# A hybrid decoder layer on one core: key scales applied later, the first six up blocks reordered, weight sums of four blocks made in DRAM

## The chip, the cores and the metric

The kernel runs on one core of a Trainium2 chip. The metric is the device time of one execution in microseconds (us). The core has five engines with a program each: TensorE (PE, whose weight loads are shown apart as PEld), VectorE (DVE), ScalarE (ACT), GpSimd (POOL) and SyncE (SP). Each works through its instructions strictly in order; an instruction that waits holds up all that stand behind it on that engine. Transfers are issued from a queue of SP, ACT or POOL and run on 16 DMA engines that the queues share. [...]

## The reference

One layer on 512 tokens of width 2048, in fp32. The kernel computes all of it; these lines are the ones around the change.

```python
def rwkv7_mix(zs, ...):
    ...
    kk = (k * k_k).reshape(hd).astype(f32)
    kk = kk / jnp.maximum(jnp.sqrt(jnp.sum(kk * kk, axis=-1, keepdims=True)), 1e-12)
    ...
def conv_ffn(h, w_up, conv_w, conv_b, w_down):
    u = h @ w_up
    ...
    val, gate = jnp.split(c, 2, axis=-1)
    return (jax.nn.silu(gate) * val) @ w_down

def reference(x, ...):
    h = rms_norm(x, norm1_g[l])
    z = h @ w_in[l]
    ...
    o_rw = rwkv7_mix(...)
    o_att = swa_attention(...)
    ...
    x = x + (g_rw * p_rw + g_att * p_att) @ w_out[l]
    x = x + conv_ffn(rms_norm(x, norm2_g[l]), w_up[l], conv_w[l], conv_b[l], w_down[l])
```

## The kernel before

**Precision.** Every fp32 operand of a large product is split into a high part (an ACT copy to fp32r, `whi` for weights) and a low part (a DVE subtraction, `wlo`), and a product is made of three matmul passes: high by high, high by low, low by high.

**Stages, in order of time.** Input projection and attention (to about 310 us); eight pairs of RWKV heads, some 98 us each, with the remaining columns of the projection filling TensorE between the steps of the recurrence (to 1100); gates and branch projection (to 1329); the output projection "o" (to 1489); "up" (1490 to 2404); "down" (to 2829). The three last matrices go through a two-by-two scheme with seven products in place of eight. In "up" these are P1, P2, P7, P6, P5, Q4 and P3 for each of 44 blocks of weight columns; each product is 24 matmuls of 128x128 by 128x256. A product needs its weight as a sum of quarters of the block: s1 and s3 are sums of two quarters, P6 and P3 of three and four. It needs also its own form of the activations, a difference of the quarters q11 to q22 that is split into high and low parts on the spot (b11, b21, t3, t2, t1, t4, b22; `split_q`, L1033 to L1035).

**Weight sums in DRAM.** For "o" and "down" the sums are made in DRAM long before: `sums_along` (L226) takes a job, SP copies one quarter (L230) and POOL accumulates the other on it (L231), once per so many weight loads of the projection. For "up" the sums are made on chip: a POOL accumulate onto the loaded tile (L1056) for s1 and s3, and a DVE addition (`sums`, L1063) for P6 and P3.

**A pair of RWKV heads.** `early(p + 1)` computes the operands of the next pair while `late(p)` runs the recurrence of this one. In `early`, `head_rows` (L329) turns 8 row factors per token tile into rows that all partitions have: a PE transpose, a DVE copy to `rsT` (L332), a DMA to DRAM (`rsd`, L334) and two broadcast DMAs back (`rsb`, L338), all on SP. DVE then multiplies the keys with them (`kk`, L552). In `late`, each of the eight steps of the recurrence runs psG (PE, L731), GY (DVE, L732), psU (PE, L734), UV (ACT and DVE, L735 and L736), psS (PE, L740), SV (DVE, L744). POOL clears BAR for the next pair (L754).

**What sets the order.** Instructions are emitted under a planner that orders free ones by its own costs; those passed to `pin` keep their place. In "up" the list `steps` sets the order of the products; `run(i)` prepares the weights of product i + 2 (`prep`, which calls `parts`: whi L1069, wlo L1070), runs the matmuls of product i (L1087) and calls `out`, which moves finished sums from PSUM to `u` (ACT L1103, DVE L1105 and L1107). There are two `u` tiles for alternating blocks, and `conv` (L1121 to L1129) reads them; its parts wait in the list `later` and are handed out one or two per product.

For the first four blocks the order before is P1 of all four, P2 of all four, P7 of all four, and then the rest of blocks 0 and 1, and of 2 and 3. P1 is kept in an SBUF tile `t1`; P2 stays in the Z half of the block's X bank until `out("P2")` adds it to `t1` into `u`, after twelve products for blocks 0 and 1 and later still for 2 and 3:

```python
    for f in range(2):
        B[f].out("P2")
    for i in range(3 * NPRE, len(steps)):
        run(i)
        if steps[i] in ((2, "P6"), (2, "Q4")):
            B[2 + (steps[i][1] == "Q4")].out("P2")
```

## Time and profile before

| | |
|---|---|
| median of 3 runs | 2829.64 us (2828.12 to 2833.07) |
| profiled execution | 2830.7 us, of which the span of the instructions 2828.9 |
| mean granted TensorE clock | 0.996 |
| PE busy | 2774.4 us, 98% of the span, 17450 instructions |
| DVE, ACT, POOL busy | 1987.5 (70%), 1342.1 (47%), 225.1 (8%) |
| DMA, shares of 16 engines | SP's queue 47.1% (432.64 MB), POOL's 24.5% (132.14 MB) |

A row of a group names line, engine, operation, tiles, then the busy time, the mean of one in ns, and the idle time before it with what ended it. A row of waits names who waited for whom, the total, the number and the longest. A row of a timeline gives start, duration and instruction. "SPq" and "POOLq" are the DMA queues' issuing instructions; a transfer lands later. TensorE is the engine to follow: with 98% busy, time is won or lost where it stops or runs at a lower granted clock.

### The profile page before, as it was taken

The page shows a single profiled execution, that of the slowest core. Times are in us where ns is not written, and L with a number is a line of the kernel's source. Part 1 is how long each engine was busy: PE and PEld are TensorE (multiplying, and loading weights), DVE is VectorE, ACT ScalarE, POOL GpSimd, SP SyncE. Part 2 cuts the span into 40 slices and gives each one's busy share as a digit, 9 for nine tenths or more (in the row PEclk, how much of TensorE's full clock was granted, in tenths as well). Part 3 has the DMA queues.
Part 4 walks back from the last instruction along what each step waited for, and adds up shares of the span by engine and source line. Part 5 has one row for each costly group of instructions (what it writes and reads, how often), then busy time and mean ns, then how long its engine had stood idle before and what let it go on. Part 6 is the DMA issues. An engine that isn't in the chain of part 4 may idle for free.

```text
span 2828.9 us, 45923 instructions
## 1 busy us (share of the span) xinstructions
PE 2774.4 (98%) x17450; PEld 2403.0 (85%) x17450; DVE 1987.5 (70%) x3437; ACT 1342.1 (47%) x2256; POOL 225.1 (8%) x299
## 2 busy tenths in 40 slices
PE   7999999999999999999999899999999999999999
PEld 5777777777777777888888899999999999888887
DVE  4588677777777774545678777878787878655555
ACT  4355445444544553322465455555545555444444
POOL 0001000000000001011010011011101110000000
PEclk9999999999999999999999999999999999999999
DMA  7865766666666667878777789888988897877775
GB/s 216 227 159 163 187 167 168 175 164 158 175 162 171 160 165 223 234 248 292 237 251 211 210 235 241 229 229 227 241 236 222 228 242 228 315 245 241 256 256 190
DMA packets 223726, 607.04 MB, mean 215 GB/s; under 512 B 24448, under 2 KB 44560, under 8 KB 222480
## 3 DMA queue, kind: packets, MB, share of 16 engines
q1 hardware_dynamic: 156096, 432.64, 47.1%
q0 software_dynamic: 36064, 132.14, 24.5%
q10 hardware_dynamic: 31344, 39.31, 4.0%
q8 instruction: 137, 2.24, 0.3%
q14 instruction: 85, 0.70, 0.1%
HBM read 554.38 MB, written 174.40 MB: 258 GB/s over the span
## 4 chain that ended last, share of the span: by engine, by line
PE 87%; DVE 5%; ACT 3%; DMA 2%; issue 1%; SPq 0%; POOL 0%; ACTq 0%; DVEq 0%; POOLq 0%
PE X L1087 18%; PE X L954 11%; PE acc L256 9%; PE acc L255 9%; PE acc L257 9%; PE Y L954 9%; PE Y L1087 9%; PE Z L1087 4%; DVE wlo L241 1%; PE psS L740 1%; PE psG L731 1%; PE bulk L623 1%; PE bulk L673 1%; PE bulk L534 1%; ACT whi L240 1%
## 5 line engine op out<-in xcount | busy, mean ns | idle before, releaser
L255 PE MATMUL acc<-xhi,whi 128*128 128x512 f32 x1152 | 462.9, 402 | 1.9 <-DVE xlo L301 1.9
L257 PE MATMUL acc<-xhi,wlo 128*128 128x512 f32 x1152 | 463.8, 403 | 0.0
L256 PE MATMUL acc<-xlo,whi 128*128 128x512 f32 x1152 | 462.2, 401 | 0.0
L947 DVE TENSOR_TENSOR wlo<-raw,whi 128x1024 fp32r<-128x1024 f32 x210 | 256.9, 1224 | 205.1 <-ACT whi L946 204.9
L240 ACT ACTIVATE whi<-raw 128x512 fp32r<-128x512 f32 x352 | 220.0, 630 | 375.7 <-PE acc L256 295.1
L946 ACT ACTIVATE whi<-raw 128x1024 fp32r<-128x1024 f32 x210 | 222.8, 1061 | 290.6 <-PE X L954 152.9
L241 DVE TENSOR_TENSOR wlo<-raw,whi 128x512 fp32r<-128x512 f32 x352 | 241.3, 689 | 167.1 <-ACT whi L240 146.9
L1087 PE MATMUL X<-b,whi 128*128 128x256 f32 x1472 | 270.2, 284 | 2.3 <-DVE u L1107 0.9
L1087 PE MATMUL X<-t,whi 128*128 128x256 f32 x1408 | 259.6, 285 | 10.3 <-DVE u L1107 9.8
L1070 DVE TENSOR_TENSOR wlo<-raw,whi 128x1024 fp32r<-128x1024 f32 x176 | 215.0, 1222 | 77.6 <-ACT whi L1069 77.3
L1087 PE MATMUL Y<-t,whi 128*128 128x256 f32 x1408 | 257.1, 283 | 0.0
L255 PEld LDWEIGHTS acc<-xhi,whi 128*128 128x128 f32 x1152 | 217.6, 189 | 43.4 <-issue 2.5
L256 PEld LDWEIGHTS acc<-xlo,whi 128*128 128x128 f32 x1152 | 217.5, 189 | 41.9 <-issue 3.3
L257 PEld LDWEIGHTS acc<-xhi,wlo 128*128 128x128 f32 x1152 | 217.5, 189 | 38.3 <-issue 1.1
L1069 ACT ACTIVATE whi<-a 128x1024 fp32r<-128x1024 f32 x132 | 139.3, 1056 | 216.5 <-DVE a L1063 214.3
L1087 PEld LDWEIGHTS X<-b,whi 128*128 128x128 f32 x1472 | 230.7, 193 | 3.1 <-issue 2.4
L1087 PEld LDWEIGHTS X<-t,whi 128*128 128x128 f32 x1408 | 221.6, 194 | 10.9 <-DVE u L1107 7.2
L1087 PEld LDWEIGHTS Y<-t,whi 128*128 128x128 f32 x1408 | 219.8, 192 | 0.0
L1087 PE MATMUL X<-b,wlo 128*128 128x256 f32 x736 | 209.3, 284 | 2.1 <-DVE wlo L1070 2.1
L1070 DVE TENSOR_TENSOR wlo<-a,whi 128x1024 fp32r<-128x1024 f32 x132 | 161.7, 1226 | 67.3 <-ACT whi L1069 66.7
L1087 PE MATMUL X<-t,wlo 128*128 128x256 f32 x704 | 200.4, 285 | 0.0
L1087 PE MATMUL Y<-t,wlo 128*128 128x256 f32 x704 | 199.4, 283 | 0.0
(339 smaller groups left out, 5762.1 us busy)
## 6 DMA issues: line engine op xcount, KB each, us to landing
raw<-in_w_up_dram SPq DMA_DIRECT2D x180, 512.0 KB, 4.6
raw<-in_w_z_dram SPq DMA_DIRECT2D x288, 256.0 KB, 3.9
s_dn<-in_w_dn_dram POOLq DMA_DIRECT2D x88, 512.0 KB, 5.9
raw<-in_w_up_dram POOLq DMA_DIRECT2D x88, 512.0 KB, 8.7
raw<-s_dn SPq DMA_DIRECT2D x88, 512.0 KB, 3.8
raw<-in_w_dn_dram SPq DMA_DIRECT2D x66, 512.0 KB, 3.5
a<-in_w_up_dram SPq DMA_DIRECT2D x48, 512.0 KB, 6.9
s_dn<-in_w_dn_dram SPq DMA_DIRECT2D x44, 512.0 KB, 4.9
```

The source lines that it names most:

```text
L240: act.activation(hi, raw, AF.Copy)
L241: dve.tensor_tensor(lo, raw, hi.bitcast(F32), op=ALU.subtract)
L255: pe.matmul(acc, whi[:, j], xhi[:, k], start=first, stop=False)
L256: pe.matmul(acc, whi[:, j], xlo[:, k], start=False, stop=False)
L257: pe.matmul(acc, wlo[:, j], xhi[:, k], start=False, stop=last)
L534: pe.matmul(ps, w[:, i], ads[:, i], start=i == lo, stop=i == hi - 1)
L946: act.activation(whi, wr, AF.Copy)
L947: dve.tensor_tensor(wlo, wr, whi.bitcast(F32), op=ALU.subtract)
L954: pe.matmul(dst, l[:, q, ts], r[:, es], start=fst and j == 0, stop=lst and j == 2, skip_group_check=True)
L1069: pin(act.activation(hi, t, AF.Copy))
L1070: pin(dve.tensor_tensor(lo, t, hi.bitcast(F32), op=ALU.subtract))
L1087: pin(pe.matmul(ps, l[:, k], r[:, k], start=start and k + i == 0, stop=last and i == 2, skip_group_check=True))
```

## The change

**Weight sums of four up blocks.** For blocks 0 to 3 the four sums s3, s1, P6 and P3 are made in DRAM (`up_d`), 16 jobs in all. `up_sum` issues one job after each of the three gates of a pair: two transfers of 512 KB on POOL's queue, a plain copy and an accumulate that waits for the copy. In "up" these blocks load the finished sums with SP; their POOL accumulates and DVE additions are gone. On POOL's queue, around the first pair's gates (s1_dn and s3_dn are sums of "down", BAR the memset of L754), stood before:

```order
L231 DMA s4_o2_100<-in_w_o_dram 128x1024 x2
L231 DMA s4_o3_101<-in_w_o_dram 128x1024 x2
L231 DMA s1_dn0_102<-in_w_dn_dram 128x1024
L231 DMA s3_dn0_124<-in_w_dn_dram 128x1024
L231 DMA s1_dn0_102<-in_w_dn_dram 128x1024
L754 MEMSET BAR_2910 64x8x64 x2
L231 DMA s3_dn0_124<-in_w_dn_dram 128x1024
```

and stands now:

```order
L239 DMA s4_o2_100<-in_w_o_dram 128x1024 x2
L239 DMA s4_o3_101<-in_w_o_dram 128x1024 x2
L245 DMA s3_u0_146<-in_w_up_dram 128x1024 x2
L239 DMA s1_dn0_102<-in_w_dn_dram 128x1024
L245 DMA s1_u0_147<-in_w_up_dram 128x1024 x2
L239 DMA s3_dn0_124<-in_w_dn_dram 128x1024
L245 DMA P6_u0_148<-in_w_up_dram 128x1024
L245 DMA P6_u0_148<-s1_u0_147 128x1024
L239 DMA s1_dn0_102<-in_w_dn_dram 128x1024
L766 MEMSET BAR_2926 64x8x64 x2
L239 DMA s3_dn0_124<-in_w_dn_dram 128x1024
```

Each job's copy and accumulate stand behind a sum of "down" and ahead of the next one.

**Key scales.** The multiplication of `kk` with the row factors is pinned behind three operations of the value's path. On DVE, for pair 1, with the recurrence of pair 0 around it (kz is the key's tile, k2 and lw other operands of the pair), stood before:

```order
L744 SCALAR_TENSOR_TENSOR SV_2917<-SV_2917,ee_3240,psS_3630 64x64 x2
L583 TENSOR_SCALAR k2_4041<-lw_3883,half_175 128x512
L584 TENSOR_TENSOR k2_4041<-k2_4041,kz_3827 128x512
L732 COPY GY_2919<-psG_3659 128x128
L552 TENSOR_TENSOR kk_3830<-kk_3830,rsb_3861 128x512
L585 TENSOR_SCALAR lw_3883<-lw_3883 128x512
L736 COPY UV_2918<-psU_3663 64x64
L587 TENSOR_TENSOR kz_3827<-kk_3830,lw_3883 128x512
```

and stands now:

```order
L594 TENSOR_SCALAR k2_4056<-lw_3898,half_191 128x512
L595 TENSOR_TENSOR k2_4056<-k2_4056,kz_3843 128x512
L744 COPY GY_2935<-psG_3675 128x128
L596 TENSOR_SCALAR lw_3898<-lw_3898 128x512
L598 TENSOR_TENSOR kk_3846<-kk_3846,rsb_3877 128x512
L748 COPY UV_2934<-psU_3679 64x64
L599 TENSOR_TENSOR kz_3843<-kk_3846,lw_3898 128x512
L756 SCALAR_TENSOR_TENSOR SV_2933<-SV_2933,ee_3256,psS_3646 64x64 x2
```

The multiplication has changed places with one instruction, on `lw`; the copy of UV for the recurrence still stands right behind.

**Row factors of "o".** The first two tiles come from a pool of two buffers, the others from a new pool of three that lies in the memory the projection had.

**The first six up blocks.** P1, P2, P7 and P6 now run for all four blocks before anything else; then come P5, Q4 and P3 of 0 and 1, then P5, Q4 and P3 of 2 and 3 with P7 of 4 and 5 between them, and blocks 4 to 6 are interleaved as well. `split_q` is taken apart into `high` and `low`, which are pinned between single products. `out("P2")` adds to `t1` directly behind the product, and `place` copies `t1` to `u` later. Blocks 2 and 3 are kept "apart": X holds P1 + P6, Z takes P5 and P3, and `u` is written from PSUM only at P5, Q4 and P3. On DVE, before the first use of `u` (t1_, X_ and Y_ are the blocks' SBUF and PSUM tiles, x00 to x11 the activations' quarters), stood before:

```order
L1035 TENSOR_TENSOR b221_14937<-x11_12139,b220_14936 128x2048
L1070 TENSOR_TENSOR wlo_15333<-raw_15102,whi_15332 128x1024
L1063 TENSOR_TENSOR a11_15105<-a11_15105,raw_15168 128x1024
L1263 SCALAR_TENSOR_TENSOR x10_12138<-x00_12136,x10_12138 128x2048
L1070 TENSOR_TENSOR wlo_15365<-a11_15105,whi_15364 128x1024
L1070 TENSOR_TENSOR wlo_15396<-raw_15168,whi_15395 128x1024
L1035 TENSOR_TENSOR t41_14945<-x10_12138,t40_14944 128x2048
L1107 TENSOR_TENSOR u0_15431<-t1_14981,X_14956 128x256
L1107 TENSOR_TENSOR u1_15433<-t1_15034,X_15009 128x256
L1063 TENSOR_TENSOR a11_15236<-a11_15236,raw_15268 128x1024
```

and stands now, at the first four blocks' P2:

```order
L1086 TENSOR_TENSOR wlo_15216<-raw_14945,whi_15215 128x1024
L1117 TENSOR_TENSOR t1_15049<-t1_15049,X_15024 128x256
L1086 TENSOR_TENSOR wlo_15248<-raw_14947,whi_15247 128x1024
L1117 TENSOR_TENSOR t1_15084<-t1_15084,X_15059 128x256
L1053 TENSOR_TENSOR t31_14984<-x01_12185,t30_14983 128x2048
L1086 TENSOR_TENSOR wlo_15280<-raw_15000,whi_15279 128x1024
L1117 TENSOR_TENSOR t1_15145<-t1_15145,X_15120 128x256
L1086 TENSOR_TENSOR wlo_15311<-raw_15057,whi_15310 128x1024
L1310 SCALAR_TENSOR_TENSOR x01_12185<-x00_12184,x11_12187 128x2048
L1117 TENSOR_TENSOR t1_15212<-t1_15212,X_15187 128x256
L1086 TENSOR_TENSOR wlo_15347<-raw_15090,whi_15346 128x1024
L1053 TENSOR_TENSOR t21_14986<-x01_12185,t20_14985 128x2048
```

The addition that frees the X bank (L1107 before, L1117 now) has moved from behind the split of t4 to between the weight parts of P2 and P7, and the additions of L1063 are gone there.

```diff
+    NPRE = 4
+    up_d = {(f, n): dram.tile([P, DH], F32, name=f"{n}_u{f}") for f in range(NPRE) for n in ("s3", "s1", "P6", "P3")}
...
+    for f in range(NPRE):
+        w, t = a["w_up"][f], {n: up_d[f, n] for n in ("s3", "s1", "P6", "P3")}
+        up_jobs += [(t["s3"], w[0, 0], w[1, 0]), (t["s1"], w[1, 0], w[1, 1]), (t["P6"], w[0, 0], t["s1"]),
+                    (t["P3"], t["P6"], w[0, 1])]
...
+    def up_sum():
+        if up_jobs:
+            dst, *parts = up_jobs.pop(0)
+            for i, src in enumerate(parts):
+                pin(pool.dma_start(dst, src, accum_op=ALU.add if i else ALU.bypass, max_dma_last_dim=4096))
...
                 rb = head_rows(wk, bulk(), rs, "lg")
-                dve.tensor_tensor(kk, kk, rb, op=ALU.mult)
...
                 dve.tensor_tensor(k2, k2, kz, op=ALU.mult)
                 dve.tensor_scalar(ta, ta, 0.5, 0.5, op0=ALU.mult, op1=ALU.add)
                 kb = kz
+                pin(dve.tensor_tensor(kk, kk, rb, op=ALU.mult))
                 dve.tensor_tensor(kb, kk, ta, op=ALU.mult)
...
                 for _ in range(GATES_PER_PAIR * NK // 16):
                     emit_gate()
+                    up_sum()
...
-    hp = hps.enter_context(tc.tile_pool(name="hhlC", bufs=3, side="right", reuse_waits="tile"))
+    hp0 = hps.enter_context(tc.tile_pool(name="hhlC", bufs=2, side="right", reuse_waits="tile"))
...
+    hp = hps.enter_context(tc.tile_pool(name="hhlO", bufs=3, reuse_waits="tile"))
...
-                steps_of("o", i, acc[nm], c, hp)
+                steps_of("o", i, acc[nm], c, hp0 if i == 0 and c < 2 else hp)
...
-    def split_q(n, q):
-        hi, lo = (halves(x) for x in bq[n])
-        act.activation(hi, q, AF.Copy)
-        dve.tensor_tensor(lo, q, hi.bitcast(F32), op=ALU.subtract)
+    def high(n, q, pin=pin):
+        pin(act.activation(halves(bq[n][0]), q, AF.Copy))
+
+    def low(n, q, pin=pin):
+        hi, lo = (halves(x) for x in bq[n])
+        pin(dve.tensor_tensor(lo, q, hi.bitcast(F32), op=ALU.subtract))
...
             self.f, self.w, self.hl = f, {}, {}
+            self.apart = 2 <= f < NPRE
...
-            sync.dma_start(w[n], a["w_up"][(f, *at[n])])
-            if n in ("s3", "s1"):
+            sync.dma_start(w[n], up_d[f, n] if (f, n) in up_d else a["w_up"][(f, *at[n])])
+            if n in ("s3", "s1") and f >= NPRE:
                 pool.dma_start(w[n], a["w_up"][f, 1, int(n == "s1")], accum_op=ALU.add)
...
-            if n in ("P6", "P3"):
+            if n in ("P6", "P3") and self.f >= NPRE:
                 t = w["a11"]
                 pin(dve.tensor_tensor(t, t, w["s1" if n == "P6" else "a12"], op=ALU.add))
...
+            ps = getattr(self, "Z" if self.apart and n in ("P5", "P3") else into)
...
+            if self.f < NPRE:
+                if n == "P2":
+                    pin(dve.tensor_tensor(self.t1, self.t1, Z, op=ALU.add))
+                    return
+                if self.apart and n != "P1":
+                    if n != "P6":
+                        i, j, more = {"P5": (1, 1, (Z, Y)), "P3": (0, 1, (Z,)), "Q4": (1, 0, (Y,))}[n]
+                        u = us[self.f % 2][:, i, 2 + j * TH : 2 + (j + 1) * TH]
+                        pin(act.activation(u, X, AF.Copy))
+                        for ps in more:
+                            pin(dve.tensor_tensor(u, u, ps, op=ALU.add))
+                    return
...
-                pin(dve.tensor_tensor(u, self.t1 if n == "P2" and self.f < NPRE else u, ps, op=ALU.add))
+                pin(dve.tensor_tensor(u, u, ps, op=ALU.add))
+
+        def place(self):
+            pin(act.activation(us[self.f % 2][:, 0, 2 : 2 + TH], self.t1, AF.Copy))
...
-    steps = [(f, n) for n in ("P1", "P2", "P7") for f in pre]
-    for f in range(0, NPRE, 2):
-        steps += [(f + e, n) for e, n in ((0, "P6"), (0, "P5"), (1, "P6"), (0, "P3"), (1, "P5"), (0, "Q4"), (1, "P3"), (1, "Q4"))]
...
+    steps = [(f, n) for n in ("P1", "P2", "P7", "P6") for f in pre]
+    steps += [(0, "P5"), (1, "P5"), (0, "Q4"), (0, "P3"), (1, "Q4"), (1, "P3")]
+    steps += [(4, "P7"), (2, "P5"), (5, "P7"), (2, "Q4"), (3, "P5"), (2, "P3"), (3, "Q4"), (3, "P3")]
...
-    run(4)
-    dve.tensor_tensor(q12, q22, q12, op=ALU.subtract)
-    split_q("t3", q12)
...
+    run(3)
+    pin(dve.tensor_tensor(q12, q22, q12, op=ALU.subtract))
+    prep(6)
+    run(4)
+    high("t3", q12)
+    prep(7)
+    run(5)
+    low("t3", q12)
...
-    for f in range(2):
-        B[f].out("P2")
...
```

## The prediction

> **What bounds the kernel now.** I read the page first: TensorE's share of the span, and the chain that ended last.

> ```profile
> PE 2774.4 (98%) x17450; PEld 2403.0 (85%) x17450; DVE 1987.5 (70%) x3437; ACT 1342.1 (47%) x2256; POOL 225.1 (8%) x299
> ...
> PE 87%; DVE 5%; ACT 3%; DMA 2%; issue 1%; SPq 0%; POOL 0%; ACTq 0%; DVEq 0%; POOLq 0%
> ```

> TensorE bounds it, and the change takes no matmul away. So it can only gain where TensorE stops or is slowed, and lose where something new makes it stop. The second view is the busy time by stretches of 20 us at the start of "up" (PE, PEld, DVE, ACT, POOL busy with their counts, then the granted clock and the share of the DMA engines), the third who waited for whom there.

> ```profile
> 1500.00:1520.00 20.00, 18.52 (x157) 18.11 (x155) 16.86 (x16) 13.90 (x17) 2.57 (x3) 1.00 0.68 175
> 1520.00:1540.00 20.00, 16.12 (x121) 15.95 (x122) 18.89 (x15) 8.17 (x7) 1.01 (x3) 0.91 0.74 209
> 1540.00:1560.00 20.00, 19.53 (x163) 19.32 (x162) 13.42 (x14) 9.22 (x13) 2.59 (x3) 1.00 0.79 219
> 1560.00:1580.00 20.00, 12.96 (x89) 12.76 (x89) 13.29 (x18) 9.77 (x14) 1.00 (x2) 0.74 0.67 161
> 1580.00:1600.00 20.00, 19.06 (x159) 18.89 (x159) 15.61 (x22) 8.72 (x13) 3.31 (x4) 1.00 0.97 282
> 1600.00:1620.00 20.00, 20.00 (x169) 20.00 (x169) 17.10 (x22) 10.31 (x15) 1.73 (x2) 1.00 0.62 168
> ```
> ```profile
> PE X L1087 <- DVE u L1107: 10.7, 3, 7.0
> PE X L1087 <- DVE wlo L1070: 2.1, 1, 2.1
> PE X L1087 <- DVE x L968: 0.9, 1, 0.9
> PE X L1087 <- ACT u L1103: 0.5, 1, 0.5
> PE X L1087 <- ACT whi L1069: 0.5, 1, 0.5
> ```

> From 1600 on "up" runs 169 matmuls in 20 us, one per 0.118 us, with no idle time. In the 100 us before that it ran 689 (the five counts added) where 845 would fit: 156 x 0.118 = 18.5 us are lost, and 0.9 us more at the very start (the wait for x). Four of the five waits give 13.8 of the 18.5; the rest is the granted clock, 0.91 and 0.74 in two slices. These 19.4 us are the ceiling of what the reordered blocks can win. DVE was busy 13 to 19 us of each 20 in that stretch, so the additions of L1107 came late because they stood behind the activations' splits, or behind the reading of `u` by the convolution.

> **Up: what goes and what stays.** The waits for L1107 go: the addition that frees the bank now stands right behind P2's product, and blocks 2 and 3 need `u` only at P5. But the DVE work in front of the first 30 products must still fit under them. Durations, from the groups of that stretch:

> ```profile
> L1070 DVE TENSOR_TENSOR wlo<-raw,whi 128x1024 fp32r<-128x1024 f32 x18 | 21.8, 1221 | 4.2 <-ACT whi L1069 4.0 <-PE Y L1087 0.2
> ...
> L1063 DVE TENSOR_TENSOR a<-a,raw 128x1024 f32<-128x1024 f32 x9 | 11.0, 1218 | 1.4 <-DMA raw<-in_w_up_dram 1.4
> L1124 DVE SCALAR_TENSOR_TENSOR c<-u,par,c 128x512 f32<-128x512 f32 x14 | 10.5, 747 | 3.9 <-ACT c L1121 3.9
> ...
> L1035 DVE TENSOR_TENSOR t<-x,t 128x2048 fp32r<-128x2048 f32 x4 | 9.2, 2288 | 1.2 <-ACT t L1034 1.2
> ...
> L1025 DVE TENSOR_SCALAR x<-ps_t,par 128x256 f32<-128x256 f32 x8 | 3.4, 479 | 2.7 <-PE ps_t L1018 1.4 <-ACT x L1027 1.2
> ...
> L968 DVE SCALAR_TENSOR_TENSOR x<-X,x 128x512 f32<-128x512 f32 x4 | 2.5, 681 | 0.0
> L1243 DVE TENSOR_TENSOR x<-x,x 128x2048 f32<-128x2048 f32 x1 | 2.3, 2291 | 0.0
> ...
> L1107 DVE TENSOR_TENSOR u<-u,Y 128x256 f32<-128x256 f32 x4 | 1.7, 417 | 0.5 <-PE Y L1087 0.5
> ```
> ```profile
> DVE wlo L1070 <- ACT whi L1069: 12.4, 15, 1.7
> DVE c L1124 <- ACT c L1121: 3.9, 3, 1.7
> ```

> After the change the order of DVE has, from the last sums of "o" to product 30: 29 weight parts (29 x 1.22 = 35.4), 6 low splits (13.7), 4 differences (9.2), 8 copies of transposes (3.8), 4 sums of x (2.7), 15 additions to t1 or u (6.3), 8 steps of convolutions (6.0), and some 3 us of small ones: 80 us. The eight additions of L1063 (9.7 us) are no longer among them, and the split of b21 is, which had stood in "o". TensorE needs 30 x 24 x 0.118 = 85 us for the same products. DVE has then 5 us to spare, and it waits too: 12.4 + 3.9 us of the two rows, in a stretch of 117 us, which for 85 us is 12. If all of that came again DVE would be 7 us short, if none, nothing. But TensorE itself stood for 14.7 us of the 117, by the five waits above, and where DVE waits then, nothing is lost by it; I take 4 us, about the middle. To these come 0.9 for the start, 0.5 for whi, and one more drop of the clock like that of the slice with 0.91, 20 x 0.09 = 1.8. So 7.2 of 19.4 us stay: **up gains 12.2** (bounds: 0, if other waits fill the place; 18.5, if only the start stays).

> Four copies by `place` and ACT's copies for blocks 2 and 3 lie on ACT, busy 8 to 14 us in 20: nothing. The row factors of "o" in another pool cost nothing as long as "o"'s third tile lands before its product; up to 0.9 us, the size of its own start wait, if not. The loads of finished sums replace loads of quarters, the same number on SP; 8 accumulates less on POOL then.

> **The sums in DRAM: what they collide with.** Sixteen copies and sixteen accumulates of 512 KB move into the RWKV stage, onto POOL's queue. The issuing itself fits: a sum lands about 5.9 us after its issue, so a job holds POOL for 0.8 + 5.9 + 0.8 = 7.5 us, and POOL idled 12.9 between two sums.

> ```profile
> s_dn<-in_w_dn_dram POOLq DMA_DIRECT2D x88, 512.0 KB, 5.9
> ```
> ```profile
> 382.94 0.81 POOL L231 DMA_DIRECT2D s_dn<-in_w_dn_dram  x1 [9.34 <-DMA s_dn<-in_w_dn_dram]
> 396.65 0.81 POOL L231 DMA_DIRECT2D s_dn<-in_w_dn_dram  x1 [12.90 <-DMA s_dn<-in_w_dn_dram]
> ```

> In this gap the second job is issued, its copy at about 383.8 and its accumulate at about 389.7 (estimates from these rows), and in the same gap the row factors of pair 1 go to DRAM and back:

> ```profile
> 387.25 0.29 SPq L334 DMA_DIRECT2D rsd<-rsT  x1
> 389.36 1.12 SPq L338 DMA_DIRECT2D rsb<-rsd  x2
> ```
> ```profile
> rsb<-rsd SPq DMA_DIRECT2D x2, 128.0 KB, 3.0
> ```
> ```profile
> 394.09 0.68 DVE L552 TENSOR_TENSOR kk<-kk,rsb 128x512 f32<-128x512 f32 x1
> 394.69 0.42 DVE L585 TENSOR_SCALAR lw<-lw 128x512 f32<-128x512 f32 x1
> 395.14 0.23 DVE L736 COPY UV<-psU 64x64 f32<-64x64 f32 x1
> ```
> ```profile
> 395.42 0.30 PEld L740 LDWEIGHTS psS<-UV,W 128*128 128x128 f32 x2 [0.18 <-DVE UV L736]
> ```

> Undisturbed, rsd takes 2.1 us and rsb 3.0: landed at 392.9, and kk at 394.09 finds it there. Behind kk on DVE stands the copy of UV, and TensorE waits for that copy already now (0.18), with all later matmuls behind psS. So every us that rsb is late beyond its slack is a us of TensorE. Moving kk behind lw adds 0.42 to the slack, 1.6 in all in pair 1, and costs nothing by itself, since both stand ahead of UV either way.

> How late is rsb with POOL's transfers beside it? Pair 0 shows it, where a sum of "o" was issued 0.2 us ahead of rsb:

> ```profile
> 310.50 0.32 SPq L334 DMA_DIRECT2D rsd<-rsT  x1
> 314.89 0.48 SPq L338 DMA_DIRECT2D rsb<-rsd  x1
> ```
> ```profile
> 314.68 0.88 POOL L231 DMA_DIRECT2D s_o<-in_w_o_dram  x1 [8.61 <-DMA s_o<-s_o]
> ```
> ```profile
> 320.83 0.69 DVE L552 TENSOR_TENSOR kk<-kk,rsb 128x512 f32<-128x512 f32 x1 [3.70 <-DMA rsb<-rsd]
> ```

> From the issue of rsd to kk went 10.33 us. By that row, pair 1 has rsb at 387.25 + 10.33 = 397.58, and kk could start at 394.09 + 0.42: 3.07 us late. The last pair with a job there, pair 5, has

> ```profile
> 779.15 0.29 SPq L334 DMA_DIRECT2D rsd<-rsT  x1
> 780.72 1.12 SPq L338 DMA_DIRECT2D rsb<-rsd  x2
> ```
> ```profile
> 785.99 0.68 DVE L552 TENSOR_TENSOR kk<-kk,rsb 128x512 f32<-128x512 f32 x1
> ```

> and 779.15 + 10.33 - 786.41 = 3.07 again. POOL's order puts a job right behind the sum that precedes the row factors in pairs 1 to 5 and in no other: 5 x 3.07 = 15.4 us. The lower bound: only rsb is slowed, to the 5.9 us of pair 0 from its first issue; then 395.26 against 394.51 in pair 1, 0.8 late, and 786.62 against 786.41 in pair 5, 0.2: about 2.5 for the five. A gain is excluded, as no pair but 0 waited for rsb. I take the upper row, since a copy that is issued 3.4 us ahead of rsd stands before rsd as well. It need not come whole in every pair, and the forecast's own range goes down to two thirds of it.

> [...]

> **The sum.** +15.4 - 12.2 = +3.2, and 1.8 more for loss of clock in the stalls (a fifth of the 9.0 worked out below): +5.0. Against the profiled execution's 2830.7 this is 2835.7; it stands 1.1 above the median, so against the median of 2829.6 the forecast is 2835, on the edge of what a measurement of this kernel can tell from no change (0.2%, 5.7 us).

> **The rivals.** *The queues interleave and up's gain remains* (faster). Then RWKV loses 0 to 2.5 and up gains 12: 2818 to 2822 or, with up's gain at 7, 2825. For it: rsb's 3.0 us beside SP's own loads; against it: pair 0. It decides where the added delay of rsb stays under its slack, 1.6 us in pair 1. [...]

> *The clock falls in RWKV* (slower still). After the wait of 2.1 us for wlo, the slice's granted clock was 0.91, a loss of 1.8 us. If every stall of 3.07 does so: 5 x 1.8 = 9.0, and the sum is 15.4 + 9.0 - 12.2 = +12.2, 2842; with up's gain at 7 it is 2847. Against it: the other waits for L1107, 3.7 us in two, left the slice 1540 to 1560 at 1.00. [...]

> *Up trades one wait for another*: DVE remains the limit, its 80 us plus 12 of waits against 85, and the two effects nearly cancel with a smaller delay of rsb: 2827 to 2832.

> **How the numbers follow.** Forecast, 2830 to 2840: 0.45 (0.25 of it slower, 0.20 within 0.2%). Interleaving queues, 2817 to 2826: 0.28 (0.23 faster). The clock too, 2840 to 2848: 0.20. Cancelling: 0.07. So slower 0.25 + 0.20, within 0.2% 0.20 + 0.05 + 0.06, faster 0.23 + 0.01. The range 2820 to 2846 leaves out a tenth on each side.

> **What would show it.** In the waits of the profile after: kk waiting for rsb in pairs 1 to 5, about 3 us each, and psS waiting for UV as long; a pair of 98 us (391.9 from the rsd of pair 1 to that of pair 5, by four) grown to 101. In the stretches of "up" from 1505 on: the rows of L1107 gone, counts of matmuls nearer 169 and the clock at 1.00. The forecast is wrong if kk's waits are absent (rsb beside a copy is then as fast as without), or if the first 100 us of "up" still lose 15 us or more.

## The result, and the profile after

The changed kernel takes 2835.82 us in the median of 19 runs (2826.03 to 2845.63), the kernel before 2830.06 in as many (2825.96 to 2833.54). The ratio is 1.0019, with an interval of 1.001 to 1.0027: slower by some 5 us, on the edge of 0.2%. The profiled execution of the changed kernel took 2841.64 us, 5.8 above its median, so its terms add up to more than the medians show.

The small total hides large parts. The stages of the two profiled executions, from the first and last matmuls of each in the traces (us):

| | to the first pair's rsd | RWKV and the rest of the projection | gates, branch | "o" | "up" | "down" |
|---|---|---|---|---|---|---|
| before | 310.5 | 843.2 | 175.4 | 161.5 | 913.0 | 425.3 |
| after | 310.4 | 868.3 | 175.4 | 156.7 | 903.3 | 425.6 |
| difference | -0.1 | +25.1 | 0 | -4.8 | -9.7 | +0.3 |

RWKV lost 25.1, "up" won 9.7, and "o" won 4.8. On the page of the changed kernel DMA's share of the chain of work that ended last has doubled, from 2% to 4%, and TensorE's has fallen:

```profile
PE 2777.4 (98%) x17450; PEld 2406.4 (85%) x17450; DVE 1979.5 (70%) x3433; ACT 1343.4 (47%) x2260; POOL 239.9 (8%) x323
...
PE 84%; DVE 6%; DMA 4%; ACT 3%; issue 1%; SPq 0%; POOL 0%; ACTq 0%; DVEq 0%; POOLq 0%
```

The waits of TensorE (who waited for whom, us in total, times, longest) and, for the tile kk, what DVE waited for before it:

```profile
PE psS L752 <- DVE UV L748: 16.4, 5, 5.1
...
PE X L1103 <- ACT u L1123: 4.5, 1, 4.5
```
```profile
  DMA rsb<-rsd: 21.9, 6
```

The first line is new: before, no wait of psS for UV is among those of over 1 us. The third says why: in six pairs (pair 0 among them, as before) DVE stood at kk for the broadcast row factors. The rows of pair 5, of SP, POOL and DVE, beside those that the prediction showed of the same pair:

```profile
794.95 0.29 SPq L348 DMA_DIRECT2D rsd<-rsT  x1
799.79 1.12 SPq L352 DMA_DIRECT2D rsb<-rsd  x2
```
```profile
790.64 0.81 POOL L239 DMA_DIRECT2D s_dn<-in_w_dn_dram  x1 [4.16 <-DMA s_dn<-in_w_dn_dram]
791.38 0.61 POOL L245 DMA_DIRECT2D s_u<-in_w_up_dram  x1
799.67 0.81 POOL L245 DMA_DIRECT2D s_u<-in_w_up_dram  x1 [7.68 <-DMA s_u<-in_w_up_dram]
```
```profile
807.46 0.69 DVE L598 TENSOR_TENSOR kk<-kk,rsb 128x512 f32<-128x512 f32 x1 [5.24 <-DMA rsb<-rsd]
```

The job's copy is issued 3.6 us ahead of rsd and its accumulate 0.1 us ahead of rsb. The way of the row factors to DRAM and back, by the starts of these instructions in each pair (us):

| pair | 1 | 2 | 3 | 4 | 5 | 6 |
|---|---|---|---|---|---|---|
| rsd to rsb, before | 2.11 | 3.03 | 1.66 | 2.18 | 1.57 | 1.94 |
| rsd to rsb, after | 5.55 | 4.52 | 3.00 | 5.01 | 4.84 | 4.95 |
| rsd to kk, before | 6.84 | 6.85 | 6.85 | 6.86 | 6.84 | 6.84 |
| rsd to kk, after | 9.21 | 11.55 | 7.23 | 11.59 | 12.51 | 8.76 |
| DVE's wait for rsb at kk, after | 1.94 | 4.29 | 0 | 4.33 | 5.24 | 1.50 |
| rsb to kk, after | 3.7 | 7.0 | 4.2 | 6.6 | 7.7 | 3.8 |
| issue of the job's accumulate, counted from rsb, after | +2.0 | -0.2 | +2.8 | +0.3 | -0.1 | none |

SP waits for rsd before it issues rsb, in all six pairs (25.8 us together, 5.2 at most), so the first two lines are nearly rsd's own time. rsd is slower in all six pairs, by 1.3 to 3.4 us. The second part of the way, from rsb to kk, is long only in pairs 2, 4 and 5, and these are the pairs in which the accumulate is issued within 0.3 us of rsb.

The stalls also cost clock. The busy times by stretches (PE, PEld, DVE, ACT, POOL busy with their counts, granted clock, share of the DMA engines, GB/s) of the kernel after:

```profile
500.00:600.00 100.00, 98.31 (x627) 78.50 (x628) 73.47 (x180) 46.02 (x102) 12.16 (x17) 0.97 0.75 184
600.00:700.00 100.00, 98.16 (x640) 77.78 (x639) 74.31 (x181) 47.74 (x106) 12.15 (x17) 1.00 0.78 195
700.00:800.00 100.00, 95.25 (x617) 75.95 (x618) 72.14 (x176) 45.98 (x102) 11.67 (x17) 0.98 0.76 191
800.00:900.00 100.00, 93.70 (x598) 74.39 (x597) 71.33 (x172) 43.84 (x99) 11.29 (x16) 0.97 0.75 182
900.00:1000.00 100.00, 97.47 (x640) 77.41 (x638) 74.61 (x182) 46.89 (x104) 8.12 (x11) 1.00 0.68 168
```

and one of before, like all its others between 400 and 1000:

```profile
800.00:900.00 100.00, 98.80 (x645) 78.60 (x644) 75.44 (x184) 47.50 (x106) 8.11 (x11) 1.00 0.67 168
```

Three stretches at 0.97, 0.98 and 0.97 are 8 us of TensorE. With the 16.4 of the waits that is 24.4 of the 25.1.

In "up" the start runs nearly without a gap, until one wait:

```profile
1520.00:1540.00 20.00, 20.00 (x172) 20.00 (x171) 17.43 (x21) 10.01 (x14) 0.00 (x0) 1.00 0.42 132
1540.00:1560.00 20.00, 19.80 (x164) 19.47 (x163) 16.93 (x12) 12.65 (x13) 0.15 (x2) 1.00 0.52 164
1560.00:1580.00 20.00, 20.00 (x169) 20.00 (x168) 14.81 (x14) 12.10 (x14) 1.76 (x2) 1.00 0.88 260
1580.00:1600.00 20.00, 19.80 (x165) 19.63 (x164) 15.52 (x23) 12.51 (x19) 1.71 (x2) 1.00 0.88 240
1600.00:1620.00 20.00, 15.53 (x111) 15.32 (x111) 13.07 (x19) 8.24 (x13) 2.57 (x3) 0.83 0.77 199
```

The first four slices make 670 matmuls of the 676 that four times 169 would be. The fifth makes 111: that is the wait of 4.5 us for ACT's copy at L1123, and a clock of 0.83 behind it.

### The profile page after: what moved, and what is told of

Same layout as the page of the kernel before. It is cut to its first block, busy times and chain, and to the rows that moved or that the text cites. A ratio compares the mean times of both kernels' runs of the same rounds, so it can differ in the third digit from the quotient of the medians.

```text
span 2839.8 us, 45928 instructions
## 1 busy us (share of the span) xinstructions
PE 2777.4 (98%) x17450; PEld 2406.4 (85%) x17450; DVE 1979.5 (70%) x3433; ACT 1343.4 (47%) x2260; POOL 239.9 (8%) x323
## 4 chain that ended last, share of the span: by engine, by line
PE 84%; DVE 6%; DMA 4%; ACT 3%; issue 1%; SPq 0%; POOL 0%; ACTq 0%; DVEq 0%; POOLq 0%
PE X L1103 18%; PE X L967 10%; PE acc L270 9%; PE acc L269 9%; PE acc L271 9%; PE Y L1103 9%; PE Y L967 9%; PE Z L1103 4%; DVE wlo L255 1%; DMA rsb<-rsd 1%; PE psS L752 1%; PE bulk L635 1%; PE psG L743 1%; DMA rsd<-rsT 1%; PE bulk L685 1%
## 5 line engine op out<-in xcount | busy, mean ns | idle before, releaser
L960 DVE TENSOR_TENSOR wlo<-raw,whi 128x1024 fp32r<-128x1024 f32 x210 | 257.0, 1224 | 200.3 <-ACT whi L959 200.2
L959 ACT ACTIVATE whi<-raw 128x1024 fp32r<-128x1024 f32 x210 | 222.7, 1060 | 284.6 <-PE X L967 146.4
L1086 DVE TENSOR_TENSOR wlo<-raw,whi 128x1024 fp32r<-128x1024 f32 x184 | 224.7, 1222 | 77.6 <-ACT whi L1084 77.4
L1103 PE MATMUL X<-b,whi 128*128 128x256 f32 x1472 | 270.9, 284 | 4.5 <-ACT u L1123 4.5
L1103 PE MATMUL Y<-t,whi 128*128 128x256 f32 x1408 | 257.2, 283 | 0.2 <-DVE u L1125 0.2
L1103 PE MATMUL X<-t,whi 128*128 128x256 f32 x1408 | 257.0, 283 | 0.0
L1103 PEld LDWEIGHTS X<-b,whi 128*128 128x128 f32 x1472 | 231.3, 193 | 4.8 <-ACT u L1123 4.7
L1084 ACT ACTIVATE whi<-a 128x1024 fp32r<-128x1024 f32 x124 | 130.9, 1056 | 200.2 <-DVE a L1079 196.5
L1103 PEld LDWEIGHTS Y<-t,whi 128*128 128x128 f32 x1408 | 219.6, 192 | 0.4 <-issue 0.4
L1103 PEld LDWEIGHTS X<-t,whi 128*128 128x128 f32 x1408 | 219.6, 192 | 0.0
L1103 PE MATMUL X<-b,wlo 128*128 128x256 f32 x736 | 209.4, 285 | 0.0
L1084 ACT ACTIVATE whi<-raw 128x1024 fp32r<-128x1024 f32 x184 | 192.9, 1049 | 22.7 <-ACT whi L1084 14.6
L1103 PE MATMUL Y<-t,wlo 128*128 128x256 f32 x704 | 199.4, 283 | 0.2 <-DVE wlo L1086 0.2
L1103 PE MATMUL X<-t,wlo 128*128 128x256 f32 x704 | 199.3, 283 | 0.3 <-DVE wlo L1086 0.3
## 6 DMA issues: line engine op xcount, KB each, us to landing
raw<-in_w_up_dram SPq DMA_DIRECT2D x170, 512.0 KB, 4.4
s_dn<-in_w_dn_dram POOLq DMA_DIRECT2D x88, 512.0 KB, 6.6
raw<-s_dn SPq DMA_DIRECT2D x88, 512.0 KB, 4.1
raw<-in_w_up_dram POOLq DMA_DIRECT2D x80, 512.0 KB, 8.4
raw<-in_w_dn_dram SPq DMA_DIRECT2D x66, 512.0 KB, 4.1
s_dn<-in_w_dn_dram SPq DMA_DIRECT2D x44, 512.0 KB, 6.2
s_dn<-s_dn SPq DMA_DIRECT2D x44, 512.0 KB, 10.8
```

Of the source, the lines that this page charges most:

```text
L959: act.activation(whi, wr, AF.Copy)
L960: dve.tensor_tensor(wlo, wr, whi.bitcast(F32), op=ALU.subtract)
L1084: pin(act.activation(hi, t, AF.Copy))
L1086: return lambda: pin(dve.tensor_tensor(lo, t, hi.bitcast(F32), op=ALU.subtract))
L1103: pin(pe.matmul(ps, l[:, k], r[:, k], start=start and k + i == 0, stop=last and i == 2, skip_group_check=True))
```

## The experiments

Each kernel ran beside the kernel before on the same chip. The theory at the start was that of the prediction: the jobs' transfers hold up the row factors. Against it stood that the new place of kk or the reordered "up" costs the time by itself, and for the smaller gains that the place of the row factors of "o" in memory, and not the order of the work, is what moved "o".

### The change without its jobs

```diff
-                    up_sum()
...
-            sync.dma_start(w[n], up_d[f, n] if (f, n) in up_d else a["w_up"][(f, *at[n])])
+            sync.dma_start(w[n], a["w_up"][(f, *at[n])])
```

> The changed kernel without its sixteen jobs on POOL; blocks 0 to 3 load a plain quarter where they loaded a finished sum, so the output is not the layer's. Theory 1 (the jobs slow the row factors, and that is all of the loss): RWKV is as long as before, no key scale waits for rsb in pairs 1 to 5, and what is left are up's 9.7 us and o's 4.8 us that the two profiles show: 2830 - 14.5 = 2815 or 2816. Theory 2 (the key scales' new place costs by itself): RWKV stays 10 to 25 us longer, 2826 to 2840.

Measured: 2815.12 us (2814.72 to 2818.18), ratio 0.9947 (0.9935 to 0.996). No wait of psS for UV is left, and DVE waits for rsb at kk in pair 0 alone:

```profile
  DMA rsb<-rsd: 5.1, 1
```

RWKV takes 844.1, "up" 902.6, "o" 158.4. So all of the loss hangs on the jobs; and the rest of the change, kk's new place included, wins 0.53%.

### The jobs alone, in the kernel before

```diff
+    def up_sum():
+        if up_jobs:
+            dst, *parts = up_jobs.pop(0)
+            for i, src in enumerate(parts):
+                pin(pool.dma_start(dst, src, accum_op=ALU.add if i else ALU.bypass, max_dma_last_dim=4096))
...
+                    up_sum()
```

> The kernel before with nothing added but the sixteen jobs, whose results no one reads. Theory 1: psS waits for UV in pairs 1 to 5 as in the changed kernel, 16 to 20 us in all, and the granted clock falls in some of them: 2846 to 2856, above the changed kernel, as neither up nor o gains. Theory 2: 2830 to 2834.

Measured: 2851.62 us (2845.28 to 2865.51), ratio 1.0078 (1.0058 to 1.0099). RWKV takes 866.2, 23.0 more than before, and "up" is as before (913.4). The waits of TensorE:

```profile
PE psS L755 <- DVE UV L751: 13.9, 5, 5.3
```

The granted clock in the six stretches of 100 us from 300 to 500 and 600 to 1000 was 0.99, 0.99, 0.98, 0.99, 0.97 and 0.98, together some 10 us: 13.9 + 10 is about the 23.0. The jobs alone make the new waits and the loss of clock.

### The jobs alone, copies without accumulates

```diff
+            parts = parts[:1]
             for i, src in enumerate(parts):
```

> e2 without the sixteen accumulates: the kernel before and sixteen plain copies of 512 KB on POOL's queue. If the copy ahead of rsd does the harm (rsd landing late), half or more of e2's loss stays, 2838 to 2848; if the accumulate beside rsb does it, 2830 to 2834.

Measured: 2836.42 us (2833.79 to 2838.1), ratio 1.0022 (1.0012 to 1.0032). The waits of TensorE:

```profile
PE psS L756 <- DVE UV L752: 3.6, 3, 1.8
```

RWKV loses 7.4 instead of 23.0. The copies give about a third; the rest comes with the accumulates, some of which are issued beside rsb. The traces agree: without accumulates rsd still took 3.3 to 5.0 us in pairs 1 to 5, but from rsb to kk went 3.5 to 3.9 us in all of them, and the 6.6 to 7.7 of the table above are gone. The prediction had put the delay on the copy, which stands in front of rsd.

### The jobs two at a time, behind the third gate

```diff
                 for _ in range(GATES_PER_PAIR * NK // 16):
                     emit_gate()
-                    up_sum()
+                for _ in range(2):
+                    up_sum()
```

The same 16 jobs with the same bytes now stand two in a row in each of the eight pairs, where no row factors are under way.

> The changed kernel with its jobs two at a time behind the third gate of each of the eight pairs, so that none stands behind the sum that precedes the row factors. Theory 1 (coincidence): no wait for rsb but pair 0's, 2815 to 2818. Theory 3 (the load of 32 more transfers on the DMA engines and on POOL's queue is what costs, wherever they stand): psS or acc waits 10 to 20 us all the same, 2826 to 2836.

Measured: 2816.07 us (2811.95 to 2817.87), ratio 0.9946 (0.9935 to 0.9958): level with the kernel without jobs. DVE's wait at kk, and one stretch of the busy times:

```profile
  DMA rsb<-rsd: 3.6, 1
```
```profile
800.00:900.00 100.00, 98.77 (x648) 78.72 (x647) 75.36 (x183) 47.16 (x106) 10.86 (x15) 1.00 0.77 195
```

The DMA engines are as busy as in the changed kernel (0.77 against 0.75 in this stretch, 0.76 against 0.75 in the mean from 400 to 1000), and TensorE loses nothing. It is not the amount of traffic that costs here, but where in the pair it stands: 2816.07 us against 2835.82.

### kk at its old place

One kernel has the jobs behind the third gate, the other is the changed kernel; both have

```diff
                 rb = head_rows(wk, bulk(), rs, "lg")
+                dve.tensor_tensor(kk, kk, rb, op=ALU.mult)
...
-                pin(dve.tensor_tensor(kk, kk, rb, op=ALU.mult))
```

> e3 with the key scales back at their old place in the program. Where rsb arrives in time the order of two neighbours on DVE decides nothing: 2815 to 2818, as e3. If the new place is worth something by itself: 2 us or more above e3.

> The changed kernel with the key scales at their old place, so with the jobs beside the row factors. By the prediction's step the new place gives rsb 0.42 us more in each of five pairs: 2 us more than the changed kernel, 2836 to 2841; the waits of psS for UV together 1.5 to 2.5 us longer.

Measured, with the jobs late: 2816.61 us (2815.29 to 2821.9), ratio 0.9958 (0.9945 to 0.9972); with the change's jobs: 2837.08 (2824.89 to 2841.97), ratio 1.0021 (1.001 to 1.0032). Both intervals overlap those of the same kernel with kk moved (0.9935 to 0.9958, 1.001 to 1.0027). When rsb comes in time kk's place is worth nothing that shows; whether it wins some 2 us when rsb is late is not resolved, because the runs with rsb late lie 17 us apart with kk at its old place and 20 with it moved.

### One product moved in "up"

What ACT did in the changed kernel while TensorE stood for its copy (from 1602.9 to 1607.4):

```profile
1602.72 0.81 ACT L1152 ACTIVATE c<-u,par 128x512 f32<-128x512 f32 x1 [2.68 <-DVE u L1125]
1603.44 1.04 ACT L1084 ACTIVATE whi<-a 128x1024 fp32r<-128x1024 f32 x1
1606.43 0.63 ACT L1158 ACTIVATE c<-c 128x512 f32<-128x512 f32 x1 [1.96 <-DVE c L1155]
1606.97 0.37 ACT L1123 ACTIVATE u<-X 128x256 f32<-128x256 f32 x1
```

The copy of X that frees the bank stands behind a Silu (L1158), and that waits 1.96 us for DVE's steps of the convolution. The next product that needs the bank came too early. The edit, on top of the late jobs, puts one of block 4's products ahead of it:

```diff
-    steps += [..., (3, "Q4"), (3, "P3")]
-    steps += [(4, "P1"), (4, "P2"), ...]
+    steps += [..., (3, "Q4"), (4, "P1"), (3, "P3")]
+    steps += [(4, "P2"), ...]
```

> e3 (jobs two at a time behind the third gate) with one product moved: P1 of block 4 now stands between Q4 and P3 of block 3. In the changed kernel and in e3, P3 of block 3 waits 4.5 us for the copy of X that Q4's out makes, and the granted clock falls behind it (111 matmuls in the 20 us where 169 fit). Theory 7 (the wait is that copy, queued on ACT behind a Silu that waits for DVE): a product of 2.9 us covers most of it and the clock holds, 4 to 7 us: 2809 to 2812. If DVE is simply behind there, the wait moves to the next product: 2815 to 2817.

Measured: 2813.53 us (2808.02 to 2815.97), ratio 0.994 (0.9927 to 0.9953), the lowest median of all, 22 us below the changed kernel's. The waits between 1480 and 1640:

```profile
PE X L1104 <- ACT u L1124: 1.6, 1, 1.6
PE X L1104 <- DVE wlo L1087: 1.4, 3, 0.8
```

"up" takes 899.9 against 902.6 with late jobs alone. The wait fell from 4.5 to 1.6, but some of it came back as waits for weights, so that the gain of about 2.5 us is below what was expected; the two intervals overlap.

### Why "o" became faster

A group of the matmuls of "o" before (1350 to 1460) and after (1380 to 1490; names, then busy time and mean ns):

```profile
L954 PE MATMUL Y<-whi,hhi 128*128 128x512 f32 x92 | 36.7, 399 | 0.0
```
```profile
L967 PE MATMUL Y<-whi,hhi 128*128 128x512 f32 x91 | 35.4, 389 | 0.0
```

The same matmul, with the same weights and at a clock of 1.00 in both, is 10 ns shorter. From start to start they stand 233.3 ns apart before and 226.7 after. What the change does there is to put the row factors of "o" (`hhi` and `hlo`, the factors of the activations) into another place of SBUF. They are the stationary operand: PEld loads them 128x128 at a time (188 ns each in "o" of the changed kernel), and the weights whi and wlo are the moving one, 128x512 per matmul. The first two tiles stay on the slow side in the changed kernel too, and there the same matmul takes as long as before (1354.1 to 1365):

```profile
L967 PE MATMUL X<-whi,hhi 128*128 128x512 f32 x16 | 6.4, 399 | 0.0
```

Three edits of the kernel before try this place. The first moves the old place by 32 bytes:

```diff
+    hps.enter_context(tc.tile_pool(name="padC", bufs=1, side="right")).tile([P, 8], F32, name="padC")
```

> The kernel before with an unused tile of 32 bytes ahead of the row-factor tiles of o, which moves them from an address of 32 over a multiple of 64 bytes to a multiple of 64; nothing else changes. Theory 4 (o's 4.8 us came from where these tiles lie): matmuls of o go from 233 to 227 ns, 672 of them, 4.4 us: 2825 to 2826. Theory 5 (o gained from a later split of b21, from the pool's other waits, or from the place in memory other than this offset): 233 ns and 2830 as before.

The second is the change's own two pools:

```diff
-    hp = hps.enter_context(tc.tile_pool(name="hhlC", bufs=3, side="right", reuse_waits="tile"))
+    hp0 = hps.enter_context(tc.tile_pool(name="hhlC", bufs=2, side="right", reuse_waits="tile"))
...
+    hp = hps.enter_context(tc.tile_pool(name="hhlO", bufs=3, reuse_waits="tile"))
```

> The kernel before with one part of the change alone: o's first two row-factor tiles in a pool of two, the others in a new pool in the projection's memory (byte 109056 and up of a partition, where they lay at 176800 and up). Theory 6 (the place of the stationary operand sets the time of a matmul, the offset of 32 bytes hardly): matmuls of o at 227 instead of 233 ns from the third tile on, about 620 of them, 4.1 us: 2825 to 2826. Theory 5 (o gained from another part of the change): 233 ns and 2830.

The third moves the row factors of "down", which before run at 389 ns, to the side of SBUF where those of "o" were slow (to byte 210912 and up; "o" had 176800 and up):

```diff
-                    hp0 = pd.enter_context(tc.tile_pool(name="hhl", bufs=3, reuse_waits="tile"))
+                    hp0 = pd.enter_context(tc.tile_pool(name="hhl", bufs=3, side="right", reuse_waits="tile"))
```

> The kernel before with the row-factor tiles of down moved the other way, from byte 76288 and up to 210912 and up; TensorE's order is the same. Theory 6: down's 1848 matmuls go from 227 to 232 or 233 ns, 10 to 12 us: 2840 to 2842. If the place does not matter: 2830, and 227 ns.

Measured: 2828.72 us (2827.25 to 2831.58), ratio 0.9996 (0.9987 to 1.0004), for the first; 2829.51 (2826.51 to 2831.8), 1.0001 (0.9992 to 1.001), for the second; 2858.66 (2858.6 to 2859.37), 1.0103 (1.009 to 1.0117), for the third. The same group in "o" of the first and of the second kernel, and in "down" of the third:

```profile
L955 PE MATMUL Y<-whi,hhi 128*128 128x512 f32 x66 | 26.0, 395 | 0.0
```
```profile
L954 PE MATMUL Y<-whi,hhi 128*128 128x512 f32 x69 | 26.8, 389 | 0.0
```
```profile
L954 PE MATMUL Y<-whi,hhi 128*128 128x512 f32 x264 | 104.3, 395 | 0.0
```

The offset of 32 bytes is not it: the three passes of "o" become alike (232.4 ns apart), and no faster. The two pools are it: they give the 226.7 ns, and "o" takes 159.1. By this pitch, the time from start to start, some 620 matmuls save about 4 us, but "o" is only 2.4 us shorter (159.1 against 161.5): 0.8 go again in this kernel's own waits (0.5 for wlo, 0.3 more for x than before), the rest is not accounted for, and the total shows no gain. In the changed kernel the 4.8 us of "o" are the same 4.1 and 0.7 less of waits at its end (0.9 before, 0.2 now). The third kernel makes "down" slow in the same way, 1848 matmuls by 6.6 ns or 12 us, and adds a wait by taking the memory over from "up", 12.1 us; "down" takes 26.7 us longer in all:

```profile
PE X L954 <- ACT hhi L209: 12.1, 1, 12.1
```

So the place of the stationary operand sets the time of a matmul here. Two more kernels asked where the border lies. They spread the row factors of "down" over six places between bytes 100864 and 162304 of each partition, and over five between 162304 and 211456:

```diff
+                    pd.enter_context(tc.tile_pool(name="padD", bufs=1)).tile([P, 6144], F32, name="padD")
+                    hps6 = [pd.enter_context(tc.tile_pool(name=f"hhl_{k}", bufs=2, reuse_waits="tile")) for k in range(6)]
```

> The kernel before with down's row factors (the stationary operand) spread over six pools that lie at bytes 100864, 113152, 125440, 137728, 150016 and 162304 of a partition, taken in turn. One look, for the time of a matmul by place: what is known is 227 ns up to byte 119296 and 232 to 233 ns from 176768 on. If a boundary in the address decides, some pools have 227 ns and all above them 233; if something else of those two places does (their neighbours, the side they are allocated from), all six have 227 ns. The whole: 2830 to 2842.

> As e9, with the five pools at bytes 162304, 174592, 186880, 199168 and 211456, allocated from the left as in e9 and at multiples of 64 bytes. If a boundary in the address decides, it lies between 170496 (227 ns in e9) and 176768 (232 ns in e4): the first pool has 227 ns, the third to fifth 232 to 233, the second shows on which side it falls. If the side of the allocation or a neighbour decides, all five have 227 ns.

Measured in one run each: 2834.83 us and 2842.3, the second beside 2834.81 for the kernel before on its chip. Both have a wait of some 6 us in "down" that the new pools bring. All eleven places are fast (226 to 228 ns), and those at bytes 186880 and 199168 lie among the slow ones, which go from 176768 to 210912. There is no border.

What is left is a pattern, and not shown: in every fast place the first bytes of weights and row factors have the same remainder by 2048 (512), and in every slow place they have not (672, 640 or 2016 against the 512 of the weights). The offsets are those of the built programs. The branch projection before the change adds a point: there both operands begin at remainder 608, and matmuls of the same shape are fast (442 in the 100 us from 1150, 226 ns each), so it is the agreement of the two and not the remainder 512 itself that fits. A remainder by 256 fits all these places as well as one by 2048. No kernel that ran was made to tell these patterns from another.

## Why the prediction was right, and where it was not

The time, 2835.8 against 2835.0, is right; but RWKV, "up" and the missing term of "o" were off by 8, 2.5 and 4.8 us and offset each other in part.

**"What they collide with": right, and the runs show it.** The waits were to be at kk and at psS, 3 us each in pairs 1 to 5, and go with the jobs: they do (psS waits 16.4 us for UV in the changed kernel, 13.9 with the jobs alone, and no such row is listed without jobs or with the jobs late). Taking the ratios, the jobs' place costs 1.0019 - 0.9946 of 2830, 20.7 us; the prediction had 15.4 + 1.8. In the profiled execution it is 25.1.

**The size of a stall was wrong, and its sum right by luck.** "Pair 1 has rsb at 387.25 + 10.33" took pair 0's round trip for all. It was 7.2 to 12.5, with the average of the six pairs at 10.1. So the waits of TensorE add up to 16.4 us against a forecast of 15.4, but no pair had the stall of 3.07: DVE waited 4.3 to 5.2 us in three pairs, 1.5 and 1.9 in two, and not at all in pair 3. In the three long ones the accumulate fell together with rsb.

**"In pairs 1 to 5 and in no other": not so.** Pair 3 was spared, and pair 6 was not. In pair 6 the last job's accumulate holds the queue, and the sum of "down" behind it is issued at 897.81, 2.7 us ahead of rsd instead of 4.7. The jobs also push the sums that were there already; the prediction had left them where they were. In pair 3 the copy came late:

```profile
593.98 0.54 POOL L245 DMA_DIRECT2D P_u<-P_u  x1 [4.25 <-DMA P_u<-s_u]
```

This is the copy of a P3, which reads the sum P6 that the job ahead of it is still adding to. It waits 4.25 us for that and is issued 1.07 us behind rsd, not ahead of it; rsd took 3.0 us. In the kernel with the jobs alone the copy of pair 3 came as late (0.85 us behind rsd), and DVE waited 0.36 us. With kk at its old place it came late too, but there the sum of "down" stood 2.6 us ahead of rsd instead of 4.0, rsd took 4.4 us, and DVE waited 1.6. So a late copy alone does not spare the pair; no run tries the two apart. The prediction had not followed what the jobs themselves wait for.

**The clock was underrated.** "A fifth of the 9.0" should have been nearly all: 8 us. The rival of the falling clock was right on this, and wrong to count on each stall. The stretches behind the stalls of pairs 1 and 2:

```profile
400.00:420.00 20.00, 20.00 (x104) 16.06 (x104) 16.44 (x36) 5.11 (x12) 4.00 (x6) 1.00 0.85 207
...
500.00:520.00 20.00, 19.54 (x91) 16.07 (x92) 13.82 (x33) 3.80 (x10) 2.48 (x4) 0.84 0.73 172
```

After the 1.9 us of pair 1 (and the 1.5 of pair 6) the clock stayed at 1.00; after 4.3 to 5.2 it fell, to 0.84, 0.91 and 0.92 in the slices of 20 us there. The length of a stall alone does not decide it: in the kernel with the copies alone no wait of psS for UV was longer than 1.8 us, and the 10 us behind the one that ended at 497.5 show a clock of 0.88:

```profile
500.00:510.00 10.00, 10.00 (x47) 7.95 (x46) 7.94 (x17) 2.19 (x5) 0.78 (x2) 0.88 0.76 184
```

Before the change, 0.91 came with a wait of 2.1 us. What decides behind which of the shorter stalls the clock falls is open.

**The interleaving queues: this rival's outcome did not come.** RWKV was to lose 0 to 2.5 us; it lost 25.1 in the profiled executions. rsd took 3.0 to 5.6 us from issue to the issue of rsb, against 1.6 to 3.0 before: beside transfers of 512 KB it lost 1.3 to 3.4 us, and in pairs 2, 4 and 5 the chain of two transfers, one after the other, paid twice, with 6.6 to 7.7 us from rsb to kk against 3.7 to 4.2 in the other pairs. Whether the queues interleave is not shown by any run.

**"Up gains 12.2": it gained 9.7, for another reason.** The step "DVE would be 7 us short ... I take 4" was wrong: up to 1600 DVE was in time, with 0.5 us of waits for wlo in all. What stayed was a wait of 4.5 us for ACT, which the prediction had priced at nothing ("lie on ACT, busy 8 to 14 us in 20: nothing"). Busy shares do not show it: ACT was busy 8.24 us of the 20 in that slice; it stood 1.96 us for DVE, and what stood with it was the copy behind. The same 4.5 us stand in the kernels without jobs and with the jobs late, so the jobs have no part in it. With the clock of 0.83 (3.4 us) this one wait makes most of what is left of the 19.4.

**"The row factors of "o" in another pool cost nothing": they gained 4.8.** The prediction looked at when the tiles land, not at where. The kernel with the two pools alone shows that they make the matmuls faster, about 4 of the 4.8 us; in that kernel the whole does not gain.

**kk's new place** was priced at 0.42 us of slack per pair. The slack is there, at 0.3 us: where rsb comes in time, in the kernel with the jobs late, kk starts 7.2 us behind rsd against 6.8 before. That it saves time is not shown.

In sum: RWKV lost 8 us more than forecast, "up" gained 2.5 less, "o" gained 4.8 that was not forecast, and the profiled execution lies 5.8 above its median. Its 10.9 us above the profiled execution before are twice the forecast's 5.0; that the medians came out 5.8 apart is in part luck.

The runs of the changed kernel lie 20 us apart, those with the jobs late 6; the jobs alone spread by 20 too. So the spread comes with the collision; that it is the delay of rsb that varies from run to run is the author's estimate, as each kernel has one trace.

## What to carry to other kernels

Before transfers are moved into a stage with slack on average, find the small round trips in it on which the critical engine depends, and put the large transfers behind them: the same 16 jobs cost 20 us or nothing that shows, by their place in the pair. A copy that frees a PSUM bank must not stand in its engine's queue behind a step that itself waits for another engine: here TensorE stood 4.5 us for one, and the share of ACT, busy 8.24 us of 20, did not show it. And when a tile moves in SBUF, compare the mean duration of the matmuls that read it (here 399 ns and 389).
